# A deeper weight loader and a regrouped start of the feed-forward pairs in a two-block sequence kernel

## The chip, the cores and the metric

The kernel runs on one core of a Trainium2 chip. The metric is the device time of one execution in microseconds (us). Engines are named as the profile names them: PE is TensorE (PEld its weight loads), DVE is VectorE, ACT is ScalarE, POOL is GpSimd, SP is SyncE, which issues all DMAs here.

## The reference

Two blocks of width 1024 work on one sequence of 2048 positions in float32. Cut to what matters:

```python
# first block
xn = rmsnorm(x, norm_gain)
proj = xn @ w_in                              # 1024 x 3072
y_ssm = s5_mixer(u_ssm, ...)                  # state space scan, gelu, then y * sigmoid(y @ w_glu + b_glu)
y_ssm = y_ssm * silu(z_ssm)
y_conv = short_conv_mixer(h_conv, b_conv, c_conv, conv_w) * silu(z_conv)
x = rmsnorm(x + concat(y_ssm, y_conv) @ w_out, final_norm_gain)

# second block
sh1, sc1, g1, sh2, sc2, g2 = split(silu(c) @ w_ada + b_ada)
p = (x * (1 + sc1) + sh1) @ w_in_2            # 1024 x 3328
y_conv = conv_module(a_val, a_gate, ...)      # 31 taps, layer norm, silu
y_rec = hgrn2_mixer(rq, rf, ri, rg, ...)      # gated linear recurrence in chunks of 64
y_att = chunk_attention(aq, ak, av, rel_bias) # 4 heads, 9 chunks of 64 keys
x = layer_norm(ALPHA * x + (1 + g1) * (concat(y_conv, y_rec, y_att) @ w_out_2))
gt, up = split((x * (1 + sc2) + sh2) @ w_ffn_in_2)   # 1024 x 5632
x = layer_norm(ALPHA * x + (1 + g2) * ((silu(gt) * up) @ w_ffn_out_2))
```

## The kernel before, in words

Each large product is made of float16 parts. A weight or an activation is scaled by a power of two and split into a high and a low half; a product is then three matmuls (high by high, high by low, low by high: L417, L418, L419), each with a 128x128 weight and 512 columns. One such matmul takes 0.216 us at full clock. A "group" below is the 24 matmuls (8 blocks of the inner dimension, three each) that fill one PSUM bank.

A weight passes through three steps. `load` brings it from memory by DMA (L169, 512 KB for 128 columns). `stat` multiplies it by its row gains (L360 on POOL), squares it and sums it by rows on ACT (L410), and rounds the sums to one narrow column on DVE (L365). `split` first totals that column over the partitions by a tiny matmul with ones on PE (L373), derives the power of two from it on DVE (L354 to L356), and then makes the halves (L405 on ACT, L406 on DVE). A `Loader` drives a list of weights; one call of its `step` does at most one load, one stat and one split. `d1` and `d2` say how many weights the stat and the split stand behind the load, and `d2` also how many may be loaded ahead. The Loaders are: the first weights of the first block, its 20 further column blocks, the gate's four weights (`gw`), the output weights (`wo`, one weight of 512 columns each), nine weights for the attention (`ConvAtt`), ten for the recurrence (`Rec`), and two for the second output projection.

The feed-forward weights come as pairs (`Pair`): `load` (L1885, two DMAs of 512 KB), `scale` (two Squares L410, one cast L367) and `cut` (four subtractions on POOL, the total L373, and the splits). Feed-forward products are made of seven block products instead of eight, with sums and differences of blocks as operands. `FFN.prime` is called once for each of tiles 11 to 15 of the second output projection; a call does the loads that stand next in its list `seq`, whose entries are (step, pair), up to and including the next entry that isn't a load.

In time the stages are: the first block's input projections and scan (0 to 555 us), its gate (to 735), the first output projection with the attention's weights beside it (735 to 931), attention projections and attention (to about 1228), the recurrence with the convolution's taps on DVE (L1367, L1369; to about 1790), the second output projection (to 1990), and the feed-forward (to the end). Output projections work by tiles of 128 positions, two groups each: tile t's input is transposed by DMA (L1758, L1759), multiplied, evicted on DVE (L1079 in the first, L1835 in the second), normalised, stored, split and transposed again (L1060; L1801 and L1806). In the first one a background tick follows each group, in which a Loader makes a step. The rows L1121 and L1857 load the hidden state back for the next stage, in halves.

A scheduler orders the instructions of each engine from modelled times; each engine then runs its own list strictly in order, SP too. A buffer comes from an arena in SBUF; where there is no room, the request is tried again after another tick of the background work (`retry`), so that a weight that is held longer also moves the work behind such a request.

Of the kernel before, what the change touches and what calls it, by code (L numbers as in the profile page):

```python
# [32 lines left out]
class Arena:  # L33
    def __init__(self, ap, n, unit, slack, small=0, zone=None):
        self.small = small
        self.zone = n if zone is None else zone
        self.ap = ap
        self.unit = unit
        self.slack = slack
        self.segs = [(0, n, 0)]  # L40
        self.now = 0
        self.live = {}
# [164 lines left out]


class Loader:
    def __init__(self, ws, d1=1, d2=2):  # L210
        self.ws = ws
        self.n = [0, 0, 0]
        self.d1 = d1
        self.d2 = d2
# [1746 lines left out]
class FFN:  # L1961
# [14 lines left out]

    def prime(self):
        f = self.feed
        seq = ((0, 0), (1, 0), (0, 1), (2, 0), (1, 1), (2, 1), (0, 2), (1, 2))[:PRIME_N]
        done = [x for x in seq if f.at[x[0]] > x[1]]  # L1980
        for x in seq:
            if x not in done:
                n = f.at[x[0]]
                f.soon(x)
                if f.at[x[0]] > n and x[0] == 0:
                    continue
                break
# [291 lines left out]
PRIME_N = 8  # L2279
# [75 lines left out]
```

## Time and profile before

| what | us |
|---|---|
| three runs | 3268.93, 3273.25, 3275.31 (median 3273.25) |
| the profiled execution | 3276.22 |
| its span, first to last instruction | 3274.5 |
| PE busy | 3048.2 |
| DVE busy | 2061.5 |
| ACT busy | 1116.8 |
| POOL busy | 760.0 |
| mean granted PE clock | 0.967 |

A row of a timeline reads: start in us, duration in us, engine, line, operation, output and inputs, count; in brackets the idle time of the engine just before it and what ended that. SPq is the DMA queue of SP: its time is that of the issue, not of the transfer. A row of the waits reads: waiting line, what it waited for, us in total, how many times, the longest. One core alone runs the kernel, so there is one span and one clock.

### The profile page before, as it was taken

The numbers are of one execution on the slowest core, as the hardware profiler recorded it, in microseconds if no ns is written. First come the engines' busy times: TensorE is split into PE (matmuls) and PEld (weight loads), VectorE is DVE, ScalarE is ACT, GpSimd is POOL, SyncE is SP. The second block draws the span as 40 slices with busy tenths as digits, with TensorE's granted clock in tenths as the row PEclk, the third lists the DMA queues.
The fourth block names the chain that finished last, engine by engine and source line by source line (L and its number), as shares of the span: only waits on it lengthen the run. The fifth ranks groups of instructions, "written<-read, shape, count | busy, mean of one in ns | idle before, by whom it ended". The sixth has DMA issues, their size and how long they took to land. (4 is left out here: it accounts for less than half of the span.)

```text
span 3274.5 us, 43302 instructions
## 1 busy us (share of the span) xinstructions
PE 3048.2 (93%) x16198; PEld 1532.2 (47%) x16198; DVE 2061.5 (63%) x4895; ACT 1116.8 (34%) x1745; POOL 760.0 (23%) x801
## 2 busy tenths in 40 slices
PE   6799999979799988999999878999999999899998
PEld 4344454534345654555555433444444444344443
DVE  5577887355864469999568877555555555543322
ACT  5322222584524565221333333444443333300000
POOL 0432533023332332110120223111111121023321
PEclk9899999989899998999999989999999999999999
DMA  8734443535773754100125798222331113723220
GB/s 181 166 92 111 121 125 80 120 100 152 215 219 74 138 117 106 39 14 33 62 78 140 170 250 216 90 78 78 102 110 54 58 52 119 244 68 113 68 73 31
DMA packets 549651, 364.57 MB, mean 111 GB/s; under 512 B 290152, under 2 KB 503592, under 8 KB 545344
## 3 DMA queue, kind: packets, MB, share of 16 engines
q1 hardware_dynamic: 549440, 361.81, 41.1%
q8 instruction: 127, 2.08, 0.3%
q14 instruction: 84, 0.69, 0.1%
HBM read 216.73 MB, written 84.70 MB: 92 GB/s over the span
## 5 line engine op out<-in xcount | busy, mean ns | idle before, releaser
L417 PE MATMUL psum<-arena 128*128 128x512 f16 (+2 forms) x4272 | 1601.9, 377 | 78.6 <-DMA arena<-arena 34.4
L418 PE MATMUL psum<-arena 128*128 128x512 f16 (+2 forms) x4272 | 1602.1, 376 | 8.2 <-DMA arena<-h_d 4.2
L419 PE MATMUL psum<-arena 128*128 128x512 f16 (+2 forms) x4272 | 1598.6, 376 | 0.2 <-DVE arena L406 0.2
L360 POOL TENSOR_TENSOR arena<-arena 128x64 f32<-128x64 f32 (+5 forms) x681 | 681.8, 1025 | 2089.2 <-DVE arena L2179 336.9
L417 PEld LDWEIGHTS <-arena 128*128 128x128 f16 x4272 | 426.0, 100 | 593.1 <-issue 101.1
L418 PEld LDWEIGHTS <-arena 128*128 128x128 f16 x4272 | 424.1, 99 | 492.1 <-issue 44.3
L419 PEld LDWEIGHTS <-arena 128*128 128x128 f16 x4272 | 424.2, 99 | 488.4 <-issue 26.1
L410 ACT ACTIVATE arena<-arena 128x1024 bf16<-128x1024 f32 (+2 forms) x218 | 237.7, 1091 | 487.0 <-DVE arena L2062 153.3
L406 DVE SCALAR_TENSOR_TENSOR arena<-arena,kept 128x1024 f16<-128x1024 f32 (+2 forms) x152 | 230.4, 1538 | 130.0 <-ACT arena L405 110.4
L2005 DVE TENSOR_TENSOR arena<-arena,psum 128x512 f32<-128x512 f32 x264 | 177.8, 684 | 206.0 <-PE psum L419 150.9
L405 ACT ACTIVATE arena<-arena,kept 128x1024 f16<-128x1024 f32 (+2 forms) x152 | 174.5, 1175 | 183.0 <-DVE kept L355 62.7
L406 DVE SCALAR_TENSOR_TENSOR arena<-arena,ring 128x1024 f16<-128x1024 f32 (+1 forms) x164 | 209.7, 1302 | 42.0 <-ACT arena L405 36.2
L405 ACT ACTIVATE arena<-arena,ring 128x1024 f16<-128x1024 f32 (+1 forms) x164 | 172.2, 1082 | 168.6 <-DVE ring L355 100.4
L1369 DVE SCALAR_TENSOR_TENSOR arena<-arena 128x512 f32<-128x512 f32 x240 | 177.9, 778 | 0.3
L1551 PE MATMUL psum<-arena 128*127 128x64 f32 (+6 forms) x896 | 106.2, 264 | 22.2 <-DVE arena L1554 21.1
L1551 PEld LDWEIGHTS psum<-arena 128*127 128x127 f32 (+6 forms) x896 | 102.0, 182 | 48.4 <-DVE arena L1554 29.8
L2179 DVE SCALAR_TENSOR_TENSOR arena<-psum,kept,arena 128x512 f32<-128x512 f32 x32 | 23.3, 747 | 144.0 <-PE psum L419 144.0
L770 DVE SCALAR_TENSOR_TENSOR arena<-arena 128x128 f32<-128x128 f32 x336 | 111.6, 367 | 1.8
L2051 ACT ACTIVATE arena<-arena,kept 128x1024 f32<-128x1024 f32 x44 | 49.8, 1142 | 124.1 <-DVE arena L2005 124.1
L1289 ACT ACTIVATE arena<-arena,ring,kept 128x640 f32<-128x640 f32 (+4 forms) x64 | 54.5, 851 | 81.8 <-DVE ring L1287 73.0
L373 PE MATMUL psum<-kept,ones 128*128 128x1 bf16 x82 | 13.3, 169 | 70.4 <-DVE kept L365 49.5
L1553 DVE TENSOR_TENSOR arena<-arena 128x256 f32<-128x256 f32 x112 | 54.9, 490 | 37.4 <-PE psum L1551 35.8
(318 smaller groups left out, 2583.2 us busy)
## 6 DMA issues: line engine op xcount, KB each, us to landing
arena<-in_w_in_dram SPq DMA_DIRECT2D x50, 512.0 KB
arena<-in_w_ada_dram SPq DMA_DIRECT2D x48, 512.0 KB
arena<-in_w_ffn_in_dram SPq DMA_DIRECT2D x44, 512.0 KB
arena<-in_w_ffn_out_dram SPq DMA_DIRECT2D x44, 512.0 KB
a_d<-arena SPq DMA_DIRECT2D x88, 256.0 KB
arena<-a_d SPq DMA_DIRECT2D x40, 512.0 KB
arena<-in_x_dram SPq DMA_DIRECT2D x32, 512.0 KB
x_d<-arena SPq DMA_DIRECT2D x32, 512.0 KB
```

The costliest lines, as they stand in the source:

```text
L360: self.nc.gpsimd.tensor_tensor(out, x, y, op)
L405: self.nc.scalar.activation(hi, src, AF.Identity, scale=s)
L406: self.nc.vector.scalar_tensor_tensor(lo, src, s, hi, op0=ALU.mult, op1=ALU.subtract)
L410: self.nc.scalar.activation(junk, src, AF.Square, accum_out=ss)
L417: self.nc.tensor.matmul(ps, lh, rh, start=start and i == 0, stop=False)
L418: self.nc.tensor.matmul(ps, lh, rl, start=False, stop=False)
L419: self.nc.tensor.matmul(ps, ll, rh, start=False, stop=stop and i == n - 1)
L770: v.scalar_tensor_tensor(ac, raw[:, kb], cc[:, kb:kb + 1], ac, op0=ALU.mult, op1=ALU.add)
L1369: v.scalar_tensor_tensor(acc[:, f], src, w, acc[:, f], op0=ALU.mult, op1=ALU.add)
L1551: nc.tensor.matmul(pv[:rows, bsl], KS[:, c * P:c * P + rows], q4[:, bsl], start=True, stop=True)
L1553: v.tensor_tensor(q4, q4, Fv[:, :, 0:1].to_broadcast([P, nb, hb]), ALU.mult)
L2005: v.tensor_tensor(out, x, ps, op)
```

## The change

Loaders split a weight when three further ones have been loaded rather than two, and may load one more ahead. The list of the first feed-forward steps is reordered: pair 0 and pair 1 are both loaded in the call at tile 11, then both scaled, then both cut.

```diff
 class Loader:
-    def __init__(self, ws, d1=1, d2=2):
+    def __init__(self, ws, d1=1, d2=3):
...
     def prime(self):
         f = self.feed
-        seq = ((0, 0), (1, 0), (0, 1), (2, 0), (1, 1), (2, 1), (0, 2), (1, 2))[:PRIME_N]
+        seq = ((0, 0), (0, 1), (1, 0), (1, 1), (2, 0), (2, 1), (0, 2), (1, 2))[:PRIME_N]
```

What this makes of the engines' lists shows at three places. In the rows, `arena` is SBUF storage, names ending in `_dram` are inputs, and `y_d`, `x_d`, `h_d` are scratch tensors in memory.

On PE, in the first output projection, this piece of the difference holds the first and the last of the nine totals of the attention's weights (of the added and removed rows only the nearest are shown):

```order
+L419 LDWEIGHTS arena
+L419 MATMUL psum<-arena 128x512
 L373 LDWEIGHTS ones
 L373 MATMUL psum<-kept,ones 128x1
@@ -7154,52 +7201,4 @@
 L373 LDWEIGHTS ones
 L373 MATMUL psum<-kept,ones 128x1
-L417 LDWEIGHTS arena
-L417 MATMUL psum<-arena 128x512
```

Ahead of the first total 48 rows are added (24 matmuls and their weight loads, one group), and behind the last one the same number is taken away: all nine totals stand one group later, and the distances among them are as before. Loads and casts of these weights stay within a few evictions of their places on SP and DVE.

On SP, at the end of the attention, the list before (L1304 transposes attention weights, L1121 loads the hidden state for the recurrence, L169 loads weights):

```order
L1304 DMA_TRANSPOSE arena<-arena 128x5x128 x7
L1121 DMA arena<-h_d 128x4096 x2
L1304 DMA_TRANSPOSE arena<-arena 128x5x128 x5
L1331 DMA y_d<-arena 128x256
L169 DMA arena<-in_w_in_dram 128x8x128 x4
L169 DMA arena<-in_w_out_dram 128x8x128
L1304 DMA_TRANSPOSE arena<-arena 128x5x128 x6
L169 DMA arena<-in_w_in_dram 128x8x128
L1304 DMA_TRANSPOSE arena<-arena 128x5x128 x2
```

The same place now:

```order
L1304 DMA_TRANSPOSE arena<-arena 128x5x128 x12
L1331 DMA y_d<-arena 128x256
L1121 DMA arena<-h_d 128x4096
L1304 DMA_TRANSPOSE arena<-arena 128x5x128 x8
L1331 DMA y_d<-arena 128x256
L1304 DMA_TRANSPOSE arena<-arena 128x5x128 x2
L169 DMA arena<-in_w_in_dram 128x8x128 x3
L1331 DMA y_d<-arena 128x256
L169 DMA arena<-in_w_in_dram 128x8x128 x2
L1121 DMA arena<-h_d 128x4096
L169 DMA arena<-in_w_in_dram 128x8x128 x4
```

The two halves of the reload no longer stand together ahead of 15 of the transposes: the first stands ahead of ten, the second behind all of them and behind five weight loads. On PE the first large matmuls of the recurrence, 144 of which stood among the attention's products, now stand behind them.

On SP, at the end of the second output projection, the list before (L1806 transposes the feed-forward's input, L1743 and L1745 load a tile's inputs, L1813 and L1765 store):

```order
L1885 DMA arena<-in_w_ffn_in_dram 128x4x256
L1806 DMA_TRANSPOSE arena<-arena 128x4x128
L1806 DMA_TRANSPOSE arena<-arena 128x8x128 x4
L1765 DMA x_d<-arena 128x1024
L1743 DMA arena<-y_d 128x1024
L1745 DMA arena<-x_d 128x1024
L1758 DMA_TRANSPOSE arena<-arena 128x8x128
L1885 DMA arena<-in_w_ffn_in_dram 128x4x256
L1759 DMA_TRANSPOSE arena<-arena 128x8x128
```

and behind these, five rows on, the two loads of pair 1. Now all four stand in one row:

```order
L1765 DMA x_d<-arena 128x1024
L1806 DMA_TRANSPOSE arena<-arena 128x4x128 x2
L1806 DMA_TRANSPOSE arena<-arena 128x8x128 x4
L1885 DMA arena<-in_w_ffn_in_dram 128x4x256 x4
L1743 DMA arena<-y_d 128x1024
L1745 DMA arena<-x_d 128x1024
L1758 DMA_TRANSPOSE arena<-arena 128x8x128
L1759 DMA_TRANSPOSE arena<-arena 128x8x128
```

The loads of tile 15's inputs and the transposes of tile 14's now stand behind all four halves. On PE the total of pair 0 moves from behind tile 12 to behind tile 13, and that of pair 1 stays behind tile 14.

## The prediction

> **What bounds the kernel now.** I read the page first, then the busy times by stage, then the waits of TensorE, and last the timelines around the longest of them.
>
> ```profile
> span 3274.5 us, 43302 instructions
> PE 3048.2 (93%) x16198; PEld 1532.2 (47%) x16198; DVE 2061.5 (63%) x4895; ACT 1116.8 (34%) x1745; POOL 760.0 (23%) x801
> ```
>
> TensorE is busy for 93% of the span, and the change removes none of its work. So all that can be won are its idle 226 us and its slow stretches. By stage (window, length, then busy time and count of PE, PEld, DVE, ACT, POOL, the granted clock as a share, the DMA share, GB/s):
>
> ```profile
> 735.00:931.00 196.00, 167.70 (x752) 74.36 (x750) 140.03 (x310) 88.07 (x104) 76.34 (x47) 0.92 0.65 189
> 1790.00:1990.00 200.00, 171.17 (x841) 83.61 (x840) 172.33 (x437) 62.42 (x95) 48.25 (x34) 0.93 0.87 203
> 2100.00:3274.00 1174.00, 1156.24 (x5360) 523.37 (x5357) 575.85 (x944) 300.52 (x396) 222.31 (x117) 0.99 0.27 88
> ```
>
> From 2100 us on TensorE hardly ever waits, so a feed-forward pair that is ready earlier there gains nothing. The two out-projections, 735 to 931 and 1790 to 1990, idle 28 and 29 us. The waits of TensorE over the whole span (waiting line, releaser: us in total, times, longest) name what the change touches:
>
> ```profile
> PE psum L373 <- DVE kept L365: 49.5, 9, 12.4
> PE psum L373 <- DVE kept L367: 20.2, 3, 18.0
> PE psum L417 <- ACT arena L405: 18.8, 4, 10.5
> ```
>
> L373 is the tiny ones-matmul that totals a weight's squares. It stands in TensorE's queue among the large matmuls and waits for a one-column cast (L365 for a Loader's weight, L367 for a pair), so every large matmul behind it waits too. The change moves these totals later against the matmuls: that is its lever.
>
> **Term 1, the first out-projection (735 to 931).** All nine totals of the attention stage's weights come one group of 24 matmuls later.
>
> ```profile
> 847.21 0.16 PE L373 MATMUL psum<-kept,ones 128*128 128x1 bf16 x1 [12.37 <-DVE kept L365]
> 891.83 0.16 PE L373 MATMUL psum<-kept,ones 128*128 128x1 bf16 x1 [10.84 <-DVE kept L365]
> 904.56 0.16 PE L373 MATMUL psum<-kept,ones 128*128 128x1 bf16 x1 [5.10 <-DVE kept L365]
> ```
>
> These three waits are 28.3 us. Each would be gone if the cast came when it does now and TensorE had enough other work, but only one group (24 matmuls at 0.216 us, 5.2 us) is put ahead of the first, and between the last two totals there stands one group both before and after. So after the last blocked total there are four groups left to do instead of five: a gain of one group, provided that the casts keep their times. What holds them:
>
> ```profile
> 846.35 0.74 DVE L1079 SCALAR_TENSOR_TENSOR arena<-psum,kept,arena 128x512 f32<-128x512 f32 x1
> 847.01 0.20 DVE L365 CAST kept<-ring 128x1 bf16<-128x1 f32 x2
> 892.03 2.36 SPq L169 DMA_DIRECT2D arena<-in_w_in_dram  x2
> 904.36 0.15 DVE L365 CAST kept<-ring 128x1 bf16<-128x1 f32 x1
> ```
>
> The cast at 847.01 follows the eviction at 846.35 at once, behind which it is queued; the last weight's load leaves SP at 892.03 and its cast is at 904.36. In the new order the second, third and fourth casts still stand behind 18 evictions and the last two behind 24 and 26, while the fifth to seventh move from 19, 21, 21 to 21, 22, 22. No load moves. Bounds: 28.3 us gained if every cast stays ahead of TensorE, 0 if the evictions' chain, not TensorE, sets the end of the stage. I take -5.2, because between the last two totals nothing changes.
>
> **Term 2, the end of the second out-projection (1900 to 2040).** This one comes from the new order of the first pairs.
>
> ```profile
> 1954.11 0.16 PE L373 MATMUL psum<-kept,ones 128*128 128x1 bf16 x1 [18.01 <-DVE kept L367]
> 1954.21 0.58 PE L417 MATMUL psum<-arena 128*128 128x512 f16 x1
> 1958.00 0.40 PE L417 MATMUL psum<-arena 128*128 128x512 f16 x1
> ```
> ```profile
> 1951.38 1.06 ACT L410 ACTIVATE arena<-arena 128x1024 bf16<-128x1024 f32 x1 [10.39 <-DMA arena<-in_w_ffn_in_dram]
> 1953.74 0.31 DVE L367 TENSOR_TENSOR kept<-ring 128x1 bf16<-128x1 f32 x1 [2.35 <-ACT arena L410]
> 1934.36 0.39 SPq L1885 DMA_DIRECT2D arena<-in_w_ffn_in_dram  x1
> 1934.84 6.68 SPq L1806 DMA_TRANSPOSE arena<-arena  x5
> 1944.96 0.77 SPq L1885 DMA_DIRECT2D arena<-in_w_ffn_in_dram  x1
> 1945.82 3.34 SPq L1759 DMA_TRANSPOSE arena<-arena  x1
> 1954.49 2.69 SPq L1885 DMA_DIRECT2D arena<-in_w_ffn_in_dram  x2
> 1957.28 1.62 SPq L1758 DMA_TRANSPOSE arena<-arena  x1
> ```
>
> The 18.0 us hang on the second half of pair 0, issued at 1944.96 and squared at 1951.38 (6.4 us later); ScalarE and VectorE stand still behind it. After the change the first total stands one tile of 48 matmuls (10.4 us) later, after tile 13, so TensorE, idle since 1954.1 - 18.0 = 1936.1, reaches it at 1936 + 10.4 = 1946. All four loads go out together behind the transposes that ended at 1941.5, so the second leaves at about 1942.3, lands at about 1948.7, and the cast comes at about 1950: a wait of 4 us. Tile 14 then needs its transposed input, which now stands behind 2 MB of weights on SP and lands at perhaps 1955 (now 1945.82 and some 5 us). ScalarE splits tile 15's input behind all four Squares, so tile 15 starts at about 1967 and ends about 11 us earlier than now. That gain doesn't all reach the end:
>
> ```profile
> 2025.15 0.57 SPq L1857
> 2027.65 8.46 DMA arena<-h_d
> 2036.16 0.39 PE psum L418
> ```
>
> The chain runs from tile 15 over a row of transposes on SP to the reload of the second half's hidden state (8.46 us), for which TensorE waits at 2036. SP's gaps from the row at 1957.28 to the end of these reloads at 2029 add up to 15.7 us, and no more than these can be squeezed out of it. Between 0 (SP sets the pace) and -15.7 I take -7, near the middle: waits on SP that come from tile 15 shrink, its issue times don't.
>
> By the Trainium skill (TensorE: Matmul & The Clock Gate, part 1), the array drops to half clock after an idle window of about 3.4 us and needs about as long to recover. The trace agrees: the first nine intervals after the 18 us wait are 0.42 us instead of 0.216, 1.9 us in all, and if the remaining wait fell below that window, term 2 would be -9 instead of -7; my 4 us stays above it.
>
> **Term 3, weights of the gate and the output before the first out-projection (577 to 684).** Splits and loads come one tick later, which lets Gelu and Silu alternate more often on ScalarE.
>
> ```profile
> 678.04 1.87 PE L417 MATMUL psum<-arena 128*128 128x512 f16 x4 [10.54 <-ACT arena L405]
> 613.00:684.00 71.00, 59.58 (x274) 27.11 (x273) 19.98 (x46) 64.39 (x73) 3.49 (x1) 0.93 0.39 89
> L945 ACT ACT_TABLE_LOAD x9 | 11.5, 1283 | 0.2
> ```
>
> ScalarE is busy for 64.4 of 71 us there, and TensorE waits 10.54 us for its split. In the new order 14 table loads instead of 10 stand ahead of that split: 4 x 1.28 = 5.1 us. ScalarE's idle of 6.6 us can take them all or none, so +5.1 to 0, and I take +3.
>
> The Trainium skill (ScalarE: Activation LUTs, "What ACT_TABLE_LOAD costs") adds a drain of about 1.38 us to each switch; then four more would cost 10.6 us and this term would be about +8. The trace shows 1283 ns and an idle of 0.2 us over nine loads, so here no drain is seen outside the load.
>
> **Term 4, from the attention to the recurrence (1195 to 1500).** The Loader holds one more raw weight, so the reload of the hidden state (L1121) finds no room until the attention's last steps are written out, and moves behind them in every queue.
>
> ```profile
> 1223.58 0.92 SPq L1121 DMA_DIRECT2D arena<-h_d  x2
> 1234.75 4.75 SPq L169 DMA_DIRECT2D arena<-in_w_in_dram  x4
> 1257.40 2.53 SPq L1304 DMA_TRANSPOSE arena<-arena  x2
> 1228.00:1260.00 32.00, 24.99 (x120) 10.72 (x120) 32.00 (x62) 19.34 (x28) 10.19 (x6) 0.79 0.83 197
> 1260.00:1300.00 40.00, 37.01 (x251) 17.92 (x250) 38.53 (x86) 27.16 (x38) 4.30 (x3) 0.96 0.22 59
> 1300.00:1500.00 200.00, 189.03 (x1081) 114.24 (x1080) 186.72 (x482) 52.64 (x125) 26.92 (x15) 0.96 0.10 34
> 1251.77 0.73 DVE L1498 SCALAR_TENSOR_TENSOR arena<-psum,kept,arena 128x512 f32<-128x512 f32 x1
> 1293.54 0.74 DVE L1498 SCALAR_TENSOR_TENSOR arena<-psum,kept,arena 128x512 f32<-128x512 f32 x1
> ```
>
> Now 144 large matmuls (31 us at 0.216) run between the attention's last products. After the change they come behind them, and the second half of the reload stands behind five 512 KB weight loads. SP's transposes (L1304, the last at 1257.40), which now lose about 7 us to the reload, four weights and what follows them, end earlier, at about 1250, and the first large matmul starts at about 1252 instead of 1228. Against that VectorE is busy for all of 1228 to 1260 and 96% of the next 40 us, and has the convolution's taps to do meanwhile: 27 of them instead of 22 ahead of the first L1498, 58 instead of 56 ahead of the second. So VectorE, which sets the pace there, loses little until 1293.54. Bounds: +20 (most of TensorE's lag, 1252 against 1228, never recovered, as it is itself busy for 189 of 200 us afterwards) and -5 (the attention's tail no longer delayed by loads). I take +4, nearer VectorE's rows.
>
> **Small terms.** In the stages up to 555 us loads and squares move by one weight while no total waits there: TensorE is its own bound, 0 within 2. In the recurrence (1300 to 1790) the same work comes in a slightly other order: 0 within 5. The total of the second output weight moves ahead by 159 matmuls, and the last wait for its split, some 2 of the 18.8 us at L417 for L405, goes: -2.
>
> **The sum**: -5 - 7 + 3 + 4 - 2 = -7 us. The profiled execution took 3276.2 us with a span of 3274.5, 3 us above the median of the three runs, 3273.25; that gives about 3269 for a profile of its like and 3266 for the median. What tells a change from none here is 0.2%, 6.5 us.
>
> **The rivals.**
> - *The chain behind the totals sets the ends (no change, 3270 to 3276).* In both out-projections VectorE is busy for some 70 to 86% and SP orders everything; if evictions and transposes end when they do now, the totals' waits only change their name. For it: the casts at 847.01 and 904.36 are late for reasons that the change leaves alone. Then terms 1 and 2 are about 0 and -3, the sum about +2. 30%.
> - *The lost overlap in term 4 decides (slower, 3280 to 3287).* TensorE has 94.5% from 1300 to 1500; if it can't recover its lag, the term is +20 and the sum +9, 3282, and 5 more if term 1 also gives nothing. It becomes slower once the lag kept is above 17.5 us, or above 12.5 with term 1 at nothing. For it: 31 us of matmuls lose their cover; against: VectorE has been the later engine. 20%.
> - *The waits at the totals vanish (3240 to 3255).* One group more would have to do for 12.4 and 10.8 us; it needs the casts to come earlier, for which only the ScalarE queue of term 2 gives cause. 12%.
> - *The table loads of term 3 with the page's drain* add 5 us to the forecast, 3271: 5%, since the rows show no drain.
> - My forecast has the remaining 33%, its own range 3261 to 3269.
>
> Range: 3249 to 3283. It leaves out the upper part of the second rival and the lower part of the third. Faster than 3266.7 are the third rival (12), two thirds of the forecast (22) and a fourth of the first rival, whose terms may give a little more (8): 0.42. Slower are the second rival and the upper end of the first: 0.22. Within 0.2%: 0.36.
>
> **What the profile after would show.** Term 1: the three L373 waits 5 us shorter in sum, and the last group of that stage about 5 us earlier. Term 2: the L367 wait down from 18.0 to about 4, tile 15 ending near 1978 less what went before, and the wait for the reload near 2029. Term 3: the wait at L417 for L405 13 to 14 instead of 10.5. Term 4: the first L417 that waits for the reload at about 1252, and the second L1498 within 5 us of 1293. I am wrong if the waits for the transposed tiles take all that the totals give up, or if TensorE falls behind through the recurrence.

## The result, and the profile after

The changed kernel takes 3311.9 us (3309.9 to 3318.5, four runs) against 3274.3 us of the kernel before beside it (3268.9 to 3277.0): a ratio of 1.012, 95% interval 1.0101 to 1.014. It is slower by some 38 us, where 7 us less had been forecast, and outside the range.

The page after, the busy times by stage (columns as before) and the waits of TensorE that answer to the ones shown:

```profile
span 3311.2 us, 43341 instructions
PE 3047.1 (92%) x16198; PEld 1535.8 (46%) x16198; DVE 2056.7 (62%) x4895; ACT 1119.0 (34%) x1747; POOL 734.3 (22%) x801
```
```profile
735.00:931.00 196.00, 178.84 (x821) 80.17 (x819) 143.53 (x307) 90.63 (x105) 69.65 (x32) 0.96 0.62 177
1790.00:1990.00 200.00, 177.84 (x893) 91.00 (x892) 167.33 (x450) 64.62 (x109) 29.55 (x21) 0.95 0.83 198
2100.00:3311.00 1211.00, 1191.97 (x5528) 539.69 (x5525) 593.22 (x979) 319.99 (x422) 221.10 (x121) 0.99 0.28 89
```
```profile
PE psum L373 <- DVE kept L365: 35.0, 9, 9.5
...
PE psum L417 <- ACT arena L405: 19.7, 4, 12.0
PE psum L417 <- DMA arena<-h_d: 17.1, 3, 8.8
PE psum L417 <- ACT arena L896: 11.6, 1, 11.6
...
PE psum L373 <- DVE kept L367: 4.7, 1, 4.7
```

The busy times of PE, DVE and ACT are those of before within 0.3%, POOL's is 3% less; the 37 us are idle time of TensorE. The waits at the totals did shrink: by 14.5 us for L365, and by 14 us at the pairs of the second out-projection, where 18.0 and 1.9 us became one wait of 5.7. The list files that one under L389, a row that follows the cast L367 on VectorE at once; its 4.7 us for L367 belong to a total at 721.5 us, ahead of the first out-projection, that waited 0.3 us before. So the list of waits says that the totals' part of the change worked. What it doesn't show is when other waits came up in their place (that of L417 for the reload was 3.9 us before). For that I took single instructions that both traces have at the same count of their line and compared their starts. L656 and L774 belong to the first block's mixers, L1280 is the attention's, L1551 the recurrence's, L2005 and L2179 are evictions of the feed-forward:

| instruction (its count) | before, us | after minus before, us |
|---|---|---|
| L656 PE, first | 169.0 | -0.4 |
| L774 PE, 13th | 404.8 | +12.9 |
| L656 PE, 49th | 545.2 | +14.4 |
| L1079 DVE, first (first out-projection) | 735.3 | +16.7 |
| L1280 PE, 36th (attention) | 1043.9 | +8.7 |
| L1280 PE, 211th | 1196.7 | +9.9 |
| L1551 PE, first (recurrence) | 1302.7 | +20.0 |
| L1551 PE, 225th | 1440.3 | +34.8 |
| L1835 DVE, first (second out-projection) | 1775.9 | +36.0 |
| L2005 DVE, 34th (feed-forward) | 2103.2 | +36.1 |
| L2179 DVE, last | 3264.5 | +36.7 |

So there are four places: +14 near 400 us, -8 in the first out-projection, +25 between 1197 and 1440 us, and nothing at the second out-projection, where the new list of pairs stands.

**Near 400 us.** TensorE, ScalarE and GpSimd after the change:

```profile
410.90 0.59 PE L417 MATMUL psum<-arena 128*128 128x512 f16 x1 [11.63 <-ACT arena L896]
```
```profile
394.72 1.15 ACT L405 ACTIVATE arena<-arena,kept 128x1024 f16<-128x1024 f32 x1
407.46 0.62 ACT L647 COPY arena<-arena 64x512 f32<-64x512 f32 x1 [11.59 <-POOL arena L360]
...
410.16 2.42 ACT L896 ACTIVATE arena<-psum,kept 128x512 f32<-128x512 f32 x4
```
```profile
403.75 3.95 POOL L360 TENSOR_TENSOR arena<-arena 128x64 f32<-128x64 f32 x15
```

and ScalarE before:

```profile
376.25 0.69 ACT L896 ACTIVATE arena<-psum,kept 128x512 f32<-128x512 f32 x1 [2.80 <-PE psum L419]
...
392.78 0.69 ACT L896 ACTIVATE arena<-psum,kept 128x512 f32<-128x512 f32 x1 [4.49 <-PE psum L419]
417.84 0.62 ACT L647 COPY arena<-arena 64x512 f32<-64x512 f32 x1 [21.95 <-POOL arena L623]
```

L896 evicts the products of a column block from PSUM, L647 copies what the scan's background work needs. Before, the four evictions stood ahead of the copies. After, they stand behind them, the copies wait for GpSimd's row of 64-column products that ends at 407.7, and TensorE has no free bank. No operation is longer; two rows of one queue have changed places.

**From 1197 to 1440 us.** The two windows run from the 211th L1280 to the first L1551 and on to the 225th. Before, then after; behind each, the first large matmul of the recurrence and the reloads:

```profile
1196.70:1302.70 106.00, 86.02 (x692) 46.58 (x689) 100.47 (x228) 66.75 (x102) 28.58 (x19) 0.89 0.55 126
1302.70:1440.30 137.60, 132.15 (x760) 79.67 (x759) 127.67 (x335) 35.71 (x91) 20.32 (x11) 0.96 0.08 28
```
```profile
1228.54 0.58 PE L417 MATMUL psum<-arena 128*128 128x512 f16 x1 [3.07 <-DMA arena<-h_d]
...
1357.26 2.69 SPq L1121 DMA_DIRECT2D arena<-h_d  x2
```
```profile
1206.50:1322.60 116.10, 85.60 (x695) 48.66 (x692) 98.88 (x247) 65.95 (x100) 26.00 (x20) 0.82 0.49 110
1322.60:1475.00 152.40, 134.17 (x759) 80.27 (x758) 119.03 (x310) 34.30 (x89) 20.13 (x10) 0.94 0.09 28
```
```profile
1267.44 0.59 PE L417 MATMUL psum<-arena 128*128 128x512 f16 x1 [8.77 <-DMA arena<-h_d]
...
1379.21 0.59 PE L417 MATMUL psum<-arena 128*128 128x512 f16 x1 [5.27 <-ACT arena L1491]
1397.75 0.61 PE L417 MATMUL psum<-arena 128*128 128x512 f16 x1 [4.34 <-DMA arena<-h_d]
```
```profile
1238.08 0.38 SPq L1121 DMA_DIRECT2D arena<-h_d  x1
1259.41 1.38 SPq L1121 DMA_DIRECT2D arena<-h_d  x1
...
1387.27 0.34 SPq L1121 DMA_DIRECT2D arena<-h_d  x1
```

The busy time of TensorE differs by no more than 2 us in either window; its idle time is 10 and 13 us more. The first large matmul of the recurrence starts at 1267.4, 39 us later than before, of which 10 us are delay from the stages ahead. In the trace before, 4080 large matmuls stand ahead of the attention's last product (L1323), now 3936: the 144. The next reload of the hidden state, at 1357.26 before, now leaves at 1387.27. In both traces it leaves as soon as a large matmul (L419) has ended, so TensorE's own lag delays it: the lag isn't made up later but passed on to the second half.

### The profile page after: what moved, and what is told of

It reads as the page before. It is cut to its first block, busy times and chain, and to the rows that moved or that the text cites. A ratio compares the mean times of both kernels' runs of the same rounds, so it can differ in the third digit from the quotient of the medians.

```text
span 3311.2 us, 43341 instructions
## 1 busy us (share of the span) xinstructions
PE 3047.1 (92%) x16198; PEld 1535.8 (46%) x16198; DVE 2056.7 (62%) x4895; ACT 1119.0 (34%) x1747; POOL 734.3 (22%) x801
## 5 line engine op out<-in xcount | busy, mean ns | idle before, releaser
L417 PE MATMUL psum<-arena 128*128 128x512 f16 (+2 forms) x4272 | 1600.3, 376 | 112.7 <-DMA arena<-arena 34.5
L419 PE MATMUL psum<-arena 128*128 128x512 f16 (+2 forms) x4272 | 1595.5, 375 | 7.3 <-DMA arena<-arena 4.5
L360 POOL TENSOR_TENSOR arena<-arena 128x64 f32<-128x64 f32 (+5 forms) x681 | 657.7, 989 | 2092.6 <-DVE arena L2179 335.3
L417 PEld LDWEIGHTS <-arena 128*128 128x128 f16 x4272 | 425.2, 100 | 578.7 <-issue 70.0
L419 PEld LDWEIGHTS <-arena 128*128 128x128 f16 x4272 | 423.0, 99 | 495.1 <-issue 22.7
L2005 DVE TENSOR_TENSOR arena<-arena,psum 128x512 f32<-128x512 f32 x264 | 178.0, 684 | 223.9 <-PE psum L419 185.1
L406 DVE SCALAR_TENSOR_TENSOR arena<-arena,kept 128x1024 f16<-128x1024 f32 (+2 forms) x152 | 228.5, 1526 | 111.0 <-ACT arena L405 96.5
L405 ACT ACTIVATE arena<-arena,kept 128x1024 f16<-128x1024 f32 (+2 forms) x152 | 174.7, 1176 | 213.9 <-DVE kept L355 75.1
L406 DVE SCALAR_TENSOR_TENSOR arena<-arena,ring 128x1024 f16<-128x1024 f32 (+1 forms) x164 | 201.9, 1274 | 22.3 <-ACT arena L405 21.9
L405 ACT ACTIVATE arena<-arena,ring 128x1024 f16<-128x1024 f32 (+1 forms) x164 | 169.4, 1081 | 114.5 <-DVE ring L355 50.7
L1551 PE MATMUL psum<-arena 128*96 128x64 f32 (+6 forms) x896 | 106.4, 265 | 27.1 <-DVE arena L1554 27.1
L1551 PEld LDWEIGHTS psum<-arena 128*96 128x96 f32 (+6 forms) x896 | 102.8, 183 | 53.5 <-DVE arena L1554 25.7
L2179 DVE SCALAR_TENSOR_TENSOR arena<-psum,kept,arena 128x512 f32<-128x512 f32 x32 | 23.3, 747 | 150.3 <-PE psum L419 150.3
L2062 DVE SCALAR_TENSOR_TENSOR arena<-arena,kept 128x512 f32<-128x512 f32 x88 | 71.0, 806 | 1.6
```

What stands on the lines that cost most here:

```text
L360: self.nc.gpsimd.tensor_tensor(out, x, y, op)
L405: self.nc.scalar.activation(hi, src, AF.Identity, scale=s)
L406: self.nc.vector.scalar_tensor_tensor(lo, src, s, hi, op0=ALU.mult, op1=ALU.subtract)
L417: self.nc.tensor.matmul(ps, lh, rh, start=start and i == 0, stop=False)
L419: self.nc.tensor.matmul(ps, ll, rh, start=False, stop=stop and i == n - 1)
L1551: nc.tensor.matmul(pv[:rows, bsl], KS[:, c * P:c * P + rows], q4[:, bsl], start=True, stop=True)
```

## The experiments

Four theories of the loss were open: two rows exchanged on ScalarE; the overlap of attention and recurrence; the deeper loads themselves (more weights in flight, whatever the order); and the list of pairs. In the tables below, A is the window from the 211th L1280 to the first L1551 (106.0 us before, 116.1 after) and B the one on to the 225th L1551 (137.6 and 152.4). The kernel before ran again beside each group of experiments: its median was 3271.3 us beside 1 to 4, 3267.5 beside 5 to 8, 3268.5 beside 9 to 12 and 3262.2 beside 13 and 14. The ratios are to that run, and microseconds between experiments of different groups, or between an experiment and the changed kernel's 3311.9, are uncertain by such differences.

**1. The Loader's depth alone.**

```diff
-        seq = ((0, 0), (0, 1), (1, 0), (1, 1), ...
+        seq = ((0, 0), (1, 0), (0, 1), (2, 0), ...      # after.py with the old list
```


> The deeper Loader with the old list of the feed-forward pairs. Theory (three places: ScalarE's copies L647/L648 ahead of evictions near 400 us +13, lost overlap at the start of the recurrence +25, one group more ahead of the attention's totals -8; the list worth about nothing because what it wins at the totals is waited for later in the chain of tile 15): 3310, within 6 of the changed kernel. Rival (the list is worth the 7 us forecast for it): 3319. Rival (the list itself costs 10 us, since four loads stand ahead of tile 14's transposes): 3302.

Measured: 3313.0 us, ratio to before 1.0129 (1.0106 to 1.0153). The loss is the depth's; the list is worth nothing that shows beside an interval of this width.

**2. A larger reserve for the recurrence's Loader, in the changed kernel.** The Loader loads only while this many words stay free.

```diff
-REC_ROOM = 3500
+REC_ROOM = 5548
```


> The changed kernel with REC_ROOM 5548 instead of 3500 words: the recurrence's Loader leaves two more raw weights' worth of space free, so that the reload of the hidden state finds room and 144 large matmuls stand among the attention's products again, as before the change. Depth and list stay. Theory (the loss at the start of the recurrence comes from that lost overlap): 3288, 24 us less than the changed kernel, the first L1551 back to about its old distance from the attention's start. Rival (that loss comes from the deeper loads' transfers and squares themselves, not from the order): 3312, unchanged or slower, as weights come later.

Measured: 3300.5 us, 1.0096 (1.0077 to 1.0115). That is 11.4 us less than the change (12.5 less than experiment 1, which ran beside it, and 8 by the ratios), half of what was expected or less. In the profile, whose span is 13 us shorter, A is 112.5 and B 140.1:

```profile
1206.00:1318.50 112.50, 87.00 (x695) 48.33 (x692) 107.38 (x246) 63.65 (x99) 30.08 (x19) 0.86 0.51 108
1318.50:1458.60 140.10, 131.78 (x761) 78.93 (x760) 136.93 (x337) 35.53 (x90) 17.64 (x10) 0.96 0.08 27
```

So 16 of the 25 us in A and B come back with depth and list unchanged; the depth as such doesn't cost them. The reserve also delays loads, so this separates the depth from the order and timing that it led to, not the order from the timing. The 144 matmuls stand among the attention's products again in this trace.

**3. The copies on GpSimd, in the changed kernel.**

```diff
-        nc.scalar.copy(Hz[sl, :, g, 0], Hr[sl].rearrange("p r t h -> p r (t h)"))
-        nc.scalar.copy(Hz[sl, :, g, 1], Hi[sl].rearrange("p r t h -> p r (t h)"))
+        nc.gpsimd.tensor_copy(Hz[sl, :, g, 0], Hr[sl].rearrange("p r t h -> p r (t h)"))
+        nc.gpsimd.tensor_copy(Hz[sl, :, g, 1], Hi[sl].rearrange("p r t h -> p r (t h)"))
```


> The changed kernel with the four-fold copies L647/L648 on GpSimd instead of ScalarE, so that no copy that waits for GpSimd's chain stands ahead of evictions on ScalarE. Theory (the 13 us near 400 us are evictions L896 queued behind those copies): 3300, TensorE's wait of 11.6 us at L417 for L896 gone. Rival (the wait moves to GpSimd's or VectorE's queue): 3312, the same wait under another name.

Measured: 3302.6 us, 1.0101 (1.0082 to 1.0120), 9.3 us less than the change (10.4 less than experiment 1, 6 by the ratios). The waits of TensorE from 360 to 430 us are now these, and the 11.6 us for L896 are gone:

```profile
PE psum L417 <- DVE arena L898: 2.2, 1, 2.2
PE psum L417 <- ACT arena L630: 0.3, 1, 0.3
PE psum L656 <- DVE arena L643: 0.2, 1, 0.2
```

The trace shows the place more sharply than the total does. From the first L656 (169 us) to the 13th L774 the changed kernel loses 13.3 us against before; this one loses 0.5. But it is 6.4 us ahead of the changed kernel already at that first L656, where that one had lost nothing, and between the 13th L774 and the 49th L656 it loses 5.4 us, the changed kernel 1.5. So the 9.3 us are no clean measure of the exchange.

**4. Depth 3 for the attention's weights alone, in the kernel before.**

```diff
-        self.ws = Loader([W(256), ..., W(2944), W(3072, 256)])
+        self.ws = Loader([W(256), ..., W(2944), W(3072, 256)], d2=3)
```


> The kernel before with depth 3 for the attention's nine weights alone (all other Loaders 2, old list). Theory (one group more ahead of the totals in the first output projection gains 8 us and the other places stay as they were): 3265, 8 us less than before; the three long L373 waits there 28.3 us before, about 20 now. Rival (the gain belongs to the delay that came before it in the changed kernel, a stage that starts late waits less): 3273, no change.

Measured: 3283.6 us, 1.0045 (1.0029 to 1.0061): slower by 12 us, where the theory had it 8 faster and the rival level. The gain is there: its first L1079 is 0.4 us ahead of before, its first L1280 6.7 us, and the waits from 735 to 931 us, 28.3 us before, are

```profile
PE psum L373 <- DVE kept L365: 16.9, 3, 11.0
PE psum L417 <- DVE arena L1079: 5.2, 4, 3.1
```

But from its first L1551 (3.3 us ahead) to its first L1835 (19.9 us late) it loses 23 us and keeps 12 of them. B is 146.4 us. The rows of TensorE and VectorE in its recurrence stand in another order than before, though its own Loader was not touched.

**5. The same reserve in the kernel before.** Here it takes the overlap away instead of restoring it (diff as in 2).

> The kernel before (depth 2, old list) with REC_ROOM 5548 instead of 3500. Here the larger reserve does the reverse: the reload of the hidden state falls behind all of the attention's transposes and no large matmul stands among the attention's products, as in the changed kernel, while no Loader is deeper. Theory (the lost overlap alone costs it): 3272 + 16 to 25 = 3288 to 3297, equal to before up to 1190 us and late from the first L1498 on. Rival (the loss in the changed kernel comes from the deeper Loader's transfers): 3272, no change.

Measured: 3316.3 us, 1.0141 (1.0118 to 1.0165). Up to the 211th L1280 it is level with before (+0.2 us), at the first L1551 19.0 us late, at the 225th 37.8, at the end 40.1:

```profile
1196.90:1321.70 124.80, 90.36 (x693) 51.48 (x690) 106.19 (x250) 64.55 (x100) 28.50 (x18) 0.79 0.48 106
1321.70:1478.00 156.30, 140.33 (x759) 85.50 (x758) 106.83 (x287) 34.31 (x89) 23.36 (x12) 0.90 0.07 24
```

No Loader is deeper and no stage before is touched, so the place alone can cost as much as the whole change, and more than my theory allowed it. Of the 37.5 us that A and B lose, 25 are idle time of TensorE, which is the theory's upper end; the other 12.5 are longer busy time, at a granted clock of 0.79 and 0.90 where it was 0.89 and 0.96. It also has the same 5.3 us wait of L417 for L1491 in B as the changed kernel.

**6. The list alone, on the kernel of 5.**

> As the kernel before with REC_ROOM 5548, and with the new list of the feed-forward pairs: against that kernel only the list differs. Theory (the 13 us saved at the two totals are lost again behind tile 14's transposes and tile 15's eviction): within 4 of it, the L367 wait down from 18 to about 5 and new waits of 5 to 6 us each at L417. Rival (the forecast's 7 us): 7 less.

Measured: 3310.8 us (3308.0 to 3316.6) against 3316.3 (3309.4 to 3318.1) without the list. The medians differ by 5.4 us, the ranges overlap, and from the first L1835 to the 34th L2005 the one loses 1.8 us against before and the other 2.1. So the list gains nothing there that I can tell from run to run.

**7. The copies on GpSimd, in the kernel before** (diff as in 3).

> The kernel before (depth 2, old list) with the copies L647/L648 on GpSimd instead of ScalarE. Theory (the copies cost the changed kernel 13 us near 400 us because they stand ahead of evictions there; before they stand behind those evictions, and only the 7 us that their move won ahead of 170 us apply): 3266, 6 less than before. Rival (the move is worth the same 9.5 us whatever the order, so it explains nothing of the change): 3262.

Measured: 3265.1 us, 0.9994 (0.9979 to 1.0009): no change that shows. The interval leaves room for the theory's 6 us and none for the rival's 9.5. From the first L656 to the 13th L774 it takes 0.4 us longer than before: where the copies stand behind the evictions, their move does nothing at that place. From the first L1551 to the first L1835 its rows on TensorE and VectorE stand exactly as before, and B is 137.1 us.

**8. Both mends in the changed kernel** (diffs of 2 and 3).

> The changed kernel with both mends at once: REC_ROOM 5548 and the copies L647/L648 on GpSimd. Theory (two separate places, the losses add): 3312 - 11.5 - 9.5 = 3291. Rival (a stage that starts earlier waits longer, so the second mend brings less): 3300.

Measured: 3289.7 us, 1.0057 (1.0039 to 1.0075), as the theory of two separate places had it. Against the kernel before beside it, 22 us of the loss stay by the medians and 19 by the ratio, so some 15 to 21 of the 38 us are back. Its profile is of one of its fastest executions (span 3279.8, its runs reach from 3279.2 to 3292.3), so its windows aren't compared here.

**9. and 10. Depth 2 for the recurrence's weights, in the changed kernel, without and with the copies on GpSimd.**

```diff
-        self.ws = Loader(self.order)
+        self.ws = Loader(self.order, d2=2)
```


> The changed kernel with depth 2 for the recurrence's ten weights alone. 120 of the 144 large matmuls stand among the attention's products again. Theory (the 25 us between 1200 and 1440 us belong to that overlap, which the recurrence's own depth took away): 3287, +14 at 400 us and -8 by the attention as in the changed kernel, then no further loss up to 1440. Rival (the loss comes from the attention's weights or the stages before): 3312.

> The same, and the copies L647/L648 on GpSimd: both losses of the change taken away, its gain of 8 us at the totals kept. Theory (three separate places): 3268, level with before or 5 below it. Rival (the recurrence's order takes the gain away as it did where the attention's depth alone was changed): 3280.

Measured: 3305.4 us (1.0114, 1.0094 to 1.0135) and 3289.6 us (1.0065, 1.0044 to 1.0087). With 120 of the 144 matmuls back, A is 112.7 us, but B only fell from 152.4 to 148.7, with the 5.3 us wait for L1491 still in it. The overlap ahead of the first L1551 is thus not the whole of the 25 us. The copies are worth 16 us here, of which 3.6 are ahead of 169 us, as in experiment 3.

**11. and 12. Depth 3 elsewhere, in the kernel before.** The gate's and the attention's weights; the attention's and the recurrence's.

```diff
-    gw = Loader([Weight(...) for f in range(4)])
+    gw = Loader([Weight(...) for f in range(4)], d2=3)      # 11, with the diff of 4
-        self.ws = Loader(self.order)
+        self.ws = Loader(self.order, d2=3)                  # 12, with the diff of 4
```


> The kernel before with depth 3 for the gate's four and the attention's nine weights. The recurrence's Loader stays at 2, yet no large matmul stands among the attention's products (4704 stand ahead of its last, as in the changed kernel; 4848 where only the attention's depth is 3). Theory (the overlap decides, whatever Loader it falls to): 3284 + 25 = 3309, late from the first L1498 on. Rival (depth 3 in the recurrence's Loader is what costs): 3284, as with the attention alone.

> The kernel before with depth 3 for the attention's and the recurrence's weights. Here the overlap is kept (4848). Theory (the overlap decides): 3284, within 8 of the kernel with the attention's depth alone. Rival (depth 3 in the recurrence's Loader is what costs): 3309.

Measured: 3299.7 us (1.0097, 1.0074 to 1.0119) and 3293.1 us (1.0073, 1.0049 to 1.0097). Both lie between the theories. Without the overlap and with a Loader of depth 2, A is 120.5 and B 147.7; with the overlap and depth 3, A is 116.5 and B 154.2. The count of matmuls among the attention's products therefore doesn't decide by itself; the rest of the order does its part.

**13. and 14. The reload on another queue, in the changed kernel.**

```diff
-        k.nc.sync.dma_start(t[x].rearrange("p a b -> p (a b)"), dr_h[tb, x])
+        k.nc.scalar.dma_start(t[x].rearrange("p a b -> p (a b)"), dr_h[tb, x])      # 14: k.nc.gpsimd
```


> The changed kernel with the reloads of the hidden state (L1121) issued on ScalarE's DMA queue instead of SP's, so that the second half no longer stands behind five weight loads; the order of the large matmuls against the attention's products stays. Theory (the lost overlap is the order on TensorE, not the lateness of the reload): at most the 8.8 us of the wait at 1267 come back, 3304 to 3308. Rival (the late reload alone makes the stage late): 3290, with the first L1551 back at its distance of 106 us.

> The same reloads on GpSimd's queue. Theory: 3304 to 3308, as on ScalarE's queue, if GpSimd, which has little to do there, issues them as soon as the buffer is free; the wait of 4.3 us at the next reload (1397) goes too. Rival: 3290.

Measured: 3322.0 us (1.0182, 1.0153 to 1.0210) and 3325.4 us (1.0185, 1.0159 to 1.0210), slower than the change. On ScalarE's queue the second half leaves at 1266.17, 52.9 us after the 211th L1280, exactly as far as on SP's (1259.41). On GpSimd's it leaves 49.2 us after:

```profile
1263.07 0.33 ACTq L1121 DMA_DIRECT2D arena<-h_d  x1
1266.17 0.33 ACTq L1121 DMA_DIRECT2D arena<-h_d  x1
```
```profile
1269.48 0.57 POOL L1121 DMA_DIRECT2D arena<-h_d  x1 [8.29 <-DVE kept L356]
```

A is 116.2 and 113.0, and the added 7 and 14 us arise between 900 and 1200 us, where the attention's own reloads are. Taking the five weight loads out of the reload's way brought it forward by nothing on ScalarE's queue and by 3.7 us on GpSimd's. On GpSimd it didn't wait for its turn: the engine stood idle for 8.29 us ahead of it, by the profile for VectorE. So at most these 3.7 us can be put down to its place on SP's queue, and a reload that really comes early was not tried.

## Why the prediction was wrong

- **"In the stages up to 555 us ... 0 within 2": the first failed step, +14.4.** The prediction took "no total waits there" for proof that nothing could come. That evictions L896 had fallen behind copies L647 on ScalarE was not priced. Experiments 3 and 7 show the cause of its larger part: between the first L656 and the 13th L774 the exchange costs 13.3 us, 0.5 with the copies off ScalarE, and moving them where nothing had been exchanged changes that stretch by 0.4.
- **Term 4, "+4, nearer VectorE's rows": the second, +25.** The mechanism was named, also as a rival at +20, but the bound was taken at one lag. Window A lost 10 us, and B another 15, since the next reload and the gate products came late in turn. "VectorE, which sets the pace there" fell: it was busy for 119 us of B's 152 after, against 128 of 138 before, so it waited too. The first large matmul came at 1267.4 instead of the forecast 1252; 10 of these 15 us are delay from before. The second L1498, forecast within 5 us of 1293, came at 1314.0. Experiments 2 and 5 show that the reserve alone, which sets order and timing there, moves this place by 16 us down and 38 us up; experiments 9, 11 and 12 that the 144 matmuls aren't the whole of it. Which rows make the rest, some 11 us in B, stays open. One thing goes with B in all sixteen traces: the second half of the next reload leaves 50 to 57 us after the first L1551 where B is 137 to 140 us, 60 to 64 where it is 146 to 149, and 68 to 76 where it is 152 to 156. As such reloads were seen to wait for TensorE, that may be another sign of the lag and isn't shown to be its cause.
- **Term 1, -5.2: right in its way, and larger: -8.0.** The delay fell from 16.7 to 8.7 us, and by 7.5 us in experiment 4, which comes to that stage on time, so it isn't only that a stage that starts late waits less. Four waits for L365 add up to 16.5 us where three had 28.3. The first, 12.4 us before, is 0.4 now, more than the one group that the forecast allowed; the last grew from 5.1 to 8.5:

```profile
PE psum L373 <- DVE kept L365: 16.5, 4, 8.5
PE psum L417 <- DVE arena L1079: 0.6, 1, 0.6
```

- **Term 2, -7: the wait went as forecast, the gain didn't.** The step that failed is "that gain doesn't all reach the end", priced at half; none of it did:

```profile
1982.36 0.16 PE L373 MATMUL psum<-kept,ones 128*128 128x1 bf16 x1 [5.72 <-DVE ring L389]
1988.26 0.61 PE L417 MATMUL psum<-arena 128*128 128x512 f16 x1 [5.74 <-DMA arena<-arena]
...
2035.85 0.58 PE L417 MATMUL psum<-arena 128*128 128x512 f16 x1 [6.13 <-DVE arena L1835]
```
```profile
1975.32 2.31 SPq L1885 DMA_DIRECT2D arena<-in_w_ffn_in_dram  x4
...
1979.10 4.39 SPq L1758 DMA_TRANSPOSE arena<-arena  x1
1983.59 3.39 SPq L1759 DMA_TRANSPOSE arena<-arena  x1
```

  18.0 us at one total became 5.7 there and 5.7 for tile 14's transposes behind the four loads, as worked out. On TensorE the gain was there for a while: the delay of its large matmuls (L417 at the same count) falls from 30.2 us, at 1930.8 before, to 10.0 at 1961.3. Behind the two new waits it is 21.8 again, and 21.0 at 1984.1, still 9 us better, near the 11 that the forecast gave tile 15. VectorE then loses the rest: between its 28th and 29th L1835 the delay goes from 27.4 to 37.1 us, while splits L406 wait for ScalarE's L405 and that for GpSimd's L360; four of these, at 1956.7 to 1961.9 before, come 50 us later now. Tile 15 is evicted only at 2036.5 (2001.4 before, 35 us later, no gain left), and TensorE waits 4.0 us for the reload at 2069.7. Experiments 1 and 6 show that the list gains nothing that can be told; that this chain is the reason is read from the trace and was not tested.
- **Term 3, +3: +2.3** (14.4 to 16.7 us), with the four more table loads, but in part by luck. Between 545 and 735 us the waits of L417 for L405 grew by 1.5 us, the long one from 10.5 to 12.0, where 13 to 14 had been forecast; 4.4 us came from the total at 721.5, which no term had named. The small term of -2 failed: the last wait for L405 there is 2.2 us in both traces. The drain that the Trainium skill (ScalarE: Activation LUTs, "What ACT_TABLE_LOAD costs") adds to each load would have made term 3 about +8, an estimate; this trace doesn't bear that out, as the operation behind a load of 1283 ns starts 11 to 13 ns after it.
- **The rivals.** The second, the lost overlap, was right in its place and too small in its price, and had 20%. The first, that the totals' waits only change their name, holds for the pairs and not for the Loaders. Together, 14.4 + 2.3 - 8.0 + 26.1 + 1.2 + 0.7 from the table make the 36.7 us of the spans.

No version tried here beats the kernel before beyond doubt; the nearest, experiment 7, is level with it.

## What to carry to other kernels

Where a scheduler orders in-order queues by modelled times, a one-number change to a prefetch depth is an edit of every queue's order. Compare the full lists of all engines for exchanged rows, above all evictions that fall behind something with a long wait, before pricing the rows that the change is meant to move. And a wait that shrinks in the summary is no gain: follow one instruction's start from stage to stage and see where the delay rises and falls.

## What the runs showed that was not expected

- The reserve of 5548 words restores the overlap in the one kernel (-11 us) and destroys it in the other (+49 us against the kernel before run beside it, 3316.3 to 3267.5). Free space and time don't move in one direction here.
- A kernel whose only difference is one Loader's depth (experiment 4) wins 6 us in a stage and loses 23 in the next but one. In A and B together every kernel here that changed the order lost 9 to 38 us, and the one that left it alone (experiment 7) lost nothing.
- Executions of the kernel before lay between 3257.4 and 3277.6 us over these comparisons, 0.6%, so differences of 2 or 3 us between two medians say nothing.
